# A two-block transformer on one core: the DeltaNet gate z projected in the first two head groups, half of the branch gates in the last two, expert places in another order

## Chip, cores and metric

The kernel runs on one core of one Trainium2 chip. The metric is the device time of one execution in microseconds (us). The engines are PE (TensorE, matrix products), DVE (VectorE), ACT (ScalarE), POOL (GpSimd) and SP (SyncE, which here issues the loads).

## What is computed

A sequence of 256 tokens of width 1024 goes through two blocks, then the experts. All in fp32. The first block (a short convolution, cross attention to a memory, SwiGLU, then block attention with the same) is not touched. The second block, in which the change lies, is:

```python
h = rms_norm_2(x, g_mix[l]) * (1.0 + sc1) + sh1
proj = h @ w_in[l]
dn_qkv, dn_z, dn_b, dn_a, c_q, c_kv, k_r, gates = jnp.split(proj, split_at, axis=-1)
y_dn = gated_deltanet_branch(dn_qkv, dn_z, dn_b, dn_a, ...) @ w_o_dn[l]
...
o = rms_norm_2(o, o_gain) * jax.nn.silu(zf)          # zf is dn_z, at the end of the DeltaNet branch
...
y_mla = mla_branch(c_q, c_kv, k_r, ...) @ w_o_mla[l]
g_dn, g_mla = jnp.split(jax.nn.sigmoid(gates), N_BRANCHES, axis=-1)
merged = g_dn * y_dn + g_mla * y_mla
x = x + gt1 * (merged @ w_out[l])
h = rms_norm_2(x, g_ffn[l]) * (1.0 + sc2) + sh2
x = x + gt2 * expert_choice_ffn(h, w_router[l], w_gate[l], w_up[l], w_down[l])
```

`dn_z` is 1024 wide, `gates` 2048. Both depend on `h` alone. `z` is needed when a DeltaNet head is finished; the gates are needed when the two branches are projected and merged. There are 16 experts with three matrices of 1024 x 1024 each.

## The kernel before

**Products.** Weights come in pieces of 128 x 1024 fp32 (0.5 MB). For every piece `stream` lets SP load it into `st` (line 140, three buffers), ACT casts it to the high part `wh` (line 144, four buffers), DVE subtracts to get the low part `wl` (line 146, three buffers), and PE makes three products for each pair of operands (`mm3`, lines 169 to 171): high by high, high by low, low by high. In `steps_as` a piece is 12 matmuls of 512 columns, in `steps_ws` 24 of 256. A tile scheduler orders the instructions of every engine before the run; each engine then works through its own list in order. Instructions issued under `b.first()` get a high priority.

**The second block's front** (`block2_front`) goes through six slots. Slots 0 to 3 project a group of DeltaNet heads each (`heads(slot)`, six pieces of `w_qkv` on the PSUM bank pair "M", transposes on the pair "A"; `head_in` convolves them on DVE, line 987). From slot 2 on the DeltaNet chains of earlier groups run beside them, `dn.group`, a row of short steps that inverts the 128 x 128 triangles, on the bank pairs "N0" and "N1". Slots 4 and 5 hold the queries of the second attention and, in the kernel before, `z`: `zsteps` is eight pieces of `w_z` on "M"; `put_z` (lines 1593 and 1594) takes a tanh on ACT and one DVE instruction for each of the four results of 128 x 512.

**The back** (`block2_back`) makes the keys and values of the second attention (`mla_keys`: `w_ukn` and `w_ukv`, two pieces each), then the attention over eight heads (`staged`: scores on "M", softmax, transposes, product with the values). All 16 pieces of `w_gt` are a filler here: `b.spare` holds their steps, on bank pair "A"; `b.fill(4)` takes four steps, `staged` two before the first head and two after each scores, and `b.fill(99)` the rest.

**Then** `block2_out` projects both branches (`w_odn`, `w_oml`), merges them with the gates, applies `w_out` and makes the router's logits `lg` (line 1712). `moe` picks the tokens and streams the experts' weights: 96 chunks of 2 MB (`Chunks`, `ex<-in_w_ex`), loaded by SP into 12 places of SBUF. Nine of the places (`FIRST`) are loaded early, during the back and the projections, as the memory they share with other tiles comes free; places 6 and 7 (pool `late`) and 8 later; from chunk 12 on a place is refilled in the order `TURN` when PE has used it (L1413).

Of the kernel before, what the change touches and what calls it, by code (L numbers as in the profile page):

```python
# [1261 lines left out]
def mla_keys(b, ckv, kr, c2):  # L1262
# [12 lines left out]
    nc.scalar.copy(krT, ps[:, :T])  # L1275
    b.fill(4)
    ck = [b.xp.tile([P, 2, T], F32R, tag=f"ck{i}", name=f"ck{i}") for i in range(2)]
# [253 lines left out]
def block2_front(b, x, mod, cos, sin):  # L1531
# [63 lines left out]

    zsteps = b.steps_as(h, b.stream("w_z"), 2, put_z, tag="M")
    chains = {}
    for slot in range(6):
        todo = []
        if slot >= 2:  # L1600
            todo.append(chains[slot - 2])
        if 1 <= slot <= 4:
            chains[slot - 1] = dn.group(2 * (slot - 1), grps[slot - 1], f"N{slot % 2}")
            todo.append(itertools.islice(chains[slot - 1], 6))
        if slot == 0:
            todo.append(dn.picks())
        if slot == 4:
            todo.append(mla_compressed(b, ckv, kr, cos, sin))
        if slot < 4:
            todo.append(heads(slot))  # L1610
        else:
            todo.append(queries if slot == 5 else itertools.islice(queries, 5))
            todo.append(zsteps if slot == 5 else itertools.islice(zsteps, 4))
        for _ in itertools.zip_longest(*todo):
            pass
    for n in range(4):
        dn.gate(2 * n, zs)
    for t in range(2):
        dn.o[t] = dn.o[t].rearrange("p h e -> p (h e)")
    return h, dn.o, ckv, kr, qnT, qrT  # L1620


def block2_back(b, mod, h, ckv, kr, qnT, qrT):

    nc = b.nc
    c2 = mod.c2
    sg = slot(b, 5, [2, 2 * D])
    sg = sg[:, 0], sg[:, 1]


    def put_g(t, nb, ps):
        nc.scalar.activation(sg[t][:, nb * 512:nb * 512 + 512], ps, AF.Tanh, scale=0.5)

    b.spare = b.steps_as(h, b.stream("w_gt"), 4, put_g)
    knT, krT, v = mla_keys(b, ckv, kr, c2)
    om = mla_attention(b, qnT, qrT, knT, krT, v, (2, 2))
    b.fill(99)
    y = b.kact()
    return y, om, sg
# [75 lines left out]
def block2(b, x, mod, out, wctx):  # L1715
    nc, I = b.nc, b.I
    pool = lambda ctx, name, bufs=1: ctx.enter_context(b.tc.tile_pool(name=name, bufs=bufs, reuse_waits="tile"))
    with ExitStack() as outer:
        b.kp = pool(outer, "kp")
        with ExitStack() as ctx:  # L1720
            b.phase(ctx, {"A": 2, "M": 2, "N0": 2, "N1": 2})
            cos, sin = b.trig2
            got = block2_front(b, x, mod, cos, sin)
# [11 lines left out]
        with ExitStack() as ctx:  # L1735
            for n in (6, 7):
                chunk.late[n] = ctx.enter_context(
                    b.tc.tile_pool(name=f"late{n}", bufs=1, side="right", reuse_waits="tile"))
            b.phase(ctx, {"E": 4, "Y": 2, "T": 2})
            b.ctx = ctx  # L1740
            moe(b, x, mod, out, chunk)
# [10 lines left out]

FIRST = (11, 0, 1, 10, 2, 3, 4, 9, 5)

TURN = (11, 0, 1, 2, 3, 4, 5, 6, 7, 8)

# [13 lines left out]
class Chunks:  # L1770
# [8 lines left out]
    def load(self, n):  # L1779
        b = self.b  # L1780
        src = b.I["w_ex"][self.n]
        i, self.n = self.n, self.n + 1
        if n == 11:
            return self.halves(i, src)
        pool = self.shot if n == 9 else self.late[n] if n in (6, 7) else b.kp if n in (3, 4) else b.slots
        st = pool.tile([P, 4, D], F32, tag=f"slot{n}", name=b.nm("ex"))
# [7 lines left out]
    def halves(self, i, src):  # L1794


        b = self.b
        pool, tags = (b.xp, b.slots), ("half", "slot11a")
        if i != 12:
            pool, tags = (b.slots, b.slots), ("slot11a", "slot11b")  # L1800
        res = []
# [10 lines left out]
    def __call__(self):  # L1812
        if self.got:
            return self.got.pop(0)
        if self.n < 12:
            return self.load(self.n - 3)
        return self.load(TURN[(self.n - 12) % 10])

# [45 lines left out]
```

## Time and profile before

| | |
|---|---|
| median of 3 runs | 1716.4 us (1715.72 to 1717.51) |
| the profiled execution | 1720.11 us |
| its span, first to last instruction | 1718.4 us |
| mean granted clock of PE, share of full speed | 0.95 |
| busy: PE, DVE, ACT | 1519.5 us, 888.0 us, 662.1 us |
| weight pieces through `stream` on DVE (L146) | 350, mean 1226 ns |

The profiled execution is 1.7 us longer than its span: what lies ahead of the first and behind the last instruction. A full clock of 1.00 is 2.4 GHz, and the lower level is 1.2 GHz, so a mean of 0.87 over a stretch says that the lower level was granted for a part of it.

### The profile page before, as it was taken

What the parts mean: (1) busy time and instruction counts of PE and PEld (TensorE: products, weight loads), DVE (VectorE), ACT (ScalarE), POOL (GpSimd) and SP (SyncE); (2) the same over time, 40 slices, a digit from 0 to 9 for tenths busy, and PEclk for the clock granted to TensorE, in tenths of its full rate; (3) what the DMA queues carried; (4) which work ended last, traced back from release to release, by engine and by line L of the source; (5) the groups of instructions that cost most, each with busy time, mean ns of one, the idle gap of its engine ahead of it and who ended that gap; (6) DMA issues with size and microseconds to landing.
All of it is one profiled execution on the core that took longest, in us unless ns stands there. A gap on an engine that the chain in (4) does not pass through costs nothing.

```text
span 1718.4 us, 25491 instructions
## 1 busy us (share of the span) xinstructions
PE 1519.5 (88%) x10150; PEld 1179.4 (69%) x10150; DVE 888.0 (52%) x1631; ACT 662.1 (39%) x1203; POOL 113.4 (7%) x146
## 2 busy tenths in 40 slices
PE   7999999999999999999879999999999866655654
PEld 7989899988888879999778888868764311212111
DVE  7665688787666555555778876555651200101001
ACT  6445554445455544444645544545321100000000
POOL 0000000000100000000261431100000000000000
PEclk9999999999999999999988999999999977878788
DMA  6565498886544535665422232467769999999997
GB/s 224 189 185 172 137 305 316 315 321 224 185 146 148 159 98 175 190 187 185 139 74 78 72 98 87 139 245 267 267 250 405 425 423 427 422 421 423 428 422 310
DMA packets 82790, 416.01 MB, mean 242 GB/s; under 512 B 9968, under 2 KB 11120, under 8 KB 70768
## 3 DMA queue, kind: packets, MB, share of 16 engines
q1 hardware_dynamic: 82672, 414.40, 66.0%
q8 instruction: 79, 1.29, 0.3%
q14 instruction: 39, 0.32, 0.1%
HBM read 413.32 MB, written 1.05 MB: 241 GB/s over the span
## 4 chain that ended last, share of the span: by engine, by line
PE 23%; DMA 21%; DVE 4%; POOL 2%; ACT 1%; issue 1%; SPq 0%; DVEq 0%; POOLq 0%; ACTq 0%
DMA ex<-in_w_ex 20%; PE ps L169 4%; PE ps L170 4%; PE ps L171 4%; PE ps L1413 3%; PE ps L1521 1%; PE ps L1095 1%; DVE wl L146 1%; PE ps L1335 1%; POOL dr L1040 1%; PE ps L1123 1%; PE ps L503 0%; PE ps L1334 0%; POOL YT L1107 0%; DMA st<-in_w_gt 0%
## 5 line engine op out<-in xcount | busy, mean ns | idle before, releaser
L146 DVE TENSOR_TENSOR wl<-st,wh 128x1024 fp32r<-128x1024 f32 x350 | 428.2, 1226 | 251.8 <-PE ps L171 99.5
L144 ACT CAST wh<-st 128x1024 fp32r<-128x1024 f32 x350 | 367.2, 1051 | 423.9 <-PE ps L170 134.6
L171 PE MATMUL ps<-ah,wl 128*128 128x256 f32 x1152 | 323.6, 281 | 3.4 <-DVE wl L146 3.4
L169 PE MATMUL ps<-ah,wh 128*128 128x256 f32 x1152 | 323.1, 281 | 0.1
L170 PE MATMUL ps<-al,wh 128*128 128x256 f32 x1152 | 322.6, 280 | 0.4 <-DVE al L190 0.4
L171 PEld LDWEIGHTS ps<-ah,wl 128*128 128x128 f32 x1152 | 216.6, 188 | 5.6 <-DVE wl L146 5.4
L169 PEld LDWEIGHTS ps<-ah,wh 128*128 128x128 f32 x1152 | 216.3, 188 | 2.7 <-ACT wh L144 0.5
L170 PEld LDWEIGHTS ps<-al,wh 128*128 128x128 f32 x1152 | 216.1, 188 | 2.6 <-DVE al L190 0.6
L1413 PE MATMUL ps<-ex,slot 128*32 128x512 f32 x768 | 130.1, 809 | 92.0 <-DMA ex<-in_w_ex 92.0
L1413 PEld LDWEIGHTS ps<-ex,slot 128*32 128x32 f32 x768 | 24.6, 130 | 191.8 <-DMA ex<-in_w_ex 147.2
L1370 DVE TENSOR_TENSOR room<-room,ps 128x512 f32<-128x512 f32 x8 | 5.5, 688 | 219.5 <-PE ps L1413 219.5
L1413 PE MATMUL ps<-ex,room 128*32 128x256 f32 (+1 forms) x768 | 71.5, 509 | 37.8 <-DMA ex<-in_w_ex 37.8
L1369 ACT ACTIVATE room<-ps 128x512 f32<-128x512 f32 x8 | 4.8, 597 | 258.7 <-PE ps L1413 258.7
L169 PE MATMUL ps<-wh,ah 128*128 128x512 f32 x256 | 102.3, 400 | 0.4 <-ACT sk L351 0.4
L171 PE MATMUL ps<-wh,al 128*128 128x512 f32 x256 | 101.5, 396 | 0.0
L170 PE MATMUL ps<-wl,ah 128*128 128x512 f32 x256 | 101.4, 396 | 0.0
L1413 PEld LDWEIGHTS ps<-ex,room 128*32 128x32 f32 x768 | 25.0, 117 | 83.1 <-DMA ex<-in_w_ex 39.6
L836 DVE SCALAR_TENSOR_TENSOR sm<-sm,csil 128x1024 f32<-128x1024 f32 x48 | 58.7, 1223 | 27.0 <-DMA sm<-in_w_mod 25.3
L169 PE MATMUL ps<-wh,yh 128*128 128x512 f32 x176 | 69.6, 395 | 0.1
L170 PE MATMUL ps<-wl,yh 128*128 128x512 f32 x176 | 69.4, 394 | 0.0
L171 PE MATMUL ps<-wh,yl 128*128 128x512 f32 x176 | 69.4, 394 | 0.0
L171 PE MATMUL ps<-wh,ak 128*128 128x512 f32 (+1 forms) x160 | 64.0, 401 | 1.4 <-DVE ak L1553 1.4
(533 smaller groups left out, 2561.1 us busy)
## 6 DMA issues: line engine op xcount, KB each, us to landing
ex<-in_w_ex SPq DMA_DIRECT2D x85, 2048.0 KB, 28.3
st<-in_w_ff SPq DMA_DIRECT2D x132, 512.0 KB, 3.6
sm<-in_w_mod SPq DMA_DIRECT2D x48, 512.0 KB, 5.2
ex<-in_w_ex SPq DMA_DIRECT2D x22, 1024.0 KB, 34.3
st<-in_w_ci SPq DMA_DIRECT2D x24, 512.0 KB, 3.6
st<-in_w_qkv SPq DMA_DIRECT2D x24, 512.0 KB, 3.4
st<-in_w_mk SPq DMA_DIRECT2D x16, 512.0 KB, 3.5
st<-in_w_mv SPq DMA_DIRECT2D x16, 512.0 KB, 3.5
```

Of the source, the lines that this page charges most:

```text
L144: nc.scalar.copy(hi[:, :w], st[:, q, :w])
L146: e.tensor_tensor(lo[:, :w], st[:, q, :w], hi[:, :w].bitcast(F32), ALU.subtract)
L169: mm(ps, lh[0], rh[0], start=start, stop=False)
L170: mm(ps, lh[0], rh[1], start=False, stop=False)
L171: mm(ps, lh[1], rh[0], start=False, stop=stop)
L836: nc.vector.scalar_tensor_tensor(st, st, 1.0, self.sc, ALU.mult, ALU.mult, accum_out=m[:, k:k + 1])
L1040: nc.gpsimd.tensor_tensor(r, ms, gs, ALU.mult)
L1095: nc.tensor.matmul(ps[:, s - s0], self.pick[:, s], xs, start=True, stop=True)
L1123: nc.tensor.matmul(p2[:, m], z[:, m], n1[:, m], start=True, stop=True)
L1335: nc.tensor.matmul(sc[:, t], qrT[r, hd // 2, s], krT[r], start=False, stop=True)
L1413: b.nc.tensor.matmul(ps[32 * j:32 * j + 32], lhs[:, 32 * j:32 * j + 32], w[:, j], start=k == 0, stop=k == KC - 1)
L1521: nc.tensor.matmul(ps, x[t][:, c * P:(c + 1) * P], pk[:, h, t, s], start=t == 0, stop=t == 1)
```

## The change

`z` is projected in slots 0 and 1, four steps (pieces) in each, on the bank pair "N0", which the DeltaNet chains do not use before slot 2. The first half of the gates takes the place of `z` in slots 4 and 5, on "M". The other half stays filler in the back, now also on "M", with `fill(2)` ahead of the keys, none before the first head and one after each scores. The gates' result `sg` gets a pool of its own (`sgp`, on the right side of SBUF) from the start of block two to the end of the projections, where it had been in place 5 of the experts. So the places are reordered: eight early ones, late ones 11, 6 and 7, then 8; the place loaded in halves is 0 where it was 11; `TURN` follows.

```diff
@@ -1273,7 +1273,7 @@
         nc.tensor.transpose(ps[:, t * P:(t + 1) * P], kr2[:, t].rearrange("p a d -> p (a d)"), b.eye)
     krT = b.xp.tile([P, T], F32, tag="krT", name="krT")
     nc.scalar.copy(krT, ps[:, :T])
-    b.fill(4)
+    b.fill(2)
     ck = [b.xp.tile([P, 2, T], F32R, tag=f"ck{i}", name=f"ck{i}") for i in range(2)]
     b.transpose_in(ckv, lambda c, ps: b.split(ck[0], ck[1], ps, c2[:, 76:78]), kc=2, tag="N")
     b.proj_ws(ck, b.stream("w_ukn"), 8,
@@ -1593,7 +1593,14 @@
         nc.scalar.activation(z, ps, AF.Tanh, scale=0.5)
         nc.vector.scalar_tensor_tensor(z, z, 1.0, ps, ALU.add, ALU.mult)
 
-    zsteps = b.steps_as(h, b.stream("w_z"), 2, put_z, tag="M")
+
+    sg = b.sgp.tile([P, 2, 2 * D], F32, tag="sg", name="sg")
+
+    def put_g(t, nb, ps):
+        nc.scalar.activation(sg[:, t, nb * 512:nb * 512 + 512], ps, AF.Tanh, scale=0.5)
+
+    zsteps = b.steps_as(h, b.stream("w_z"), 2, put_z, tag="N0")
+    gsteps = b.steps_as(h, b.stream("w_gt"), 4, put_g, tag="M")
     chains = {}
     for slot in range(6):
         todo = []
@@ -1606,34 +1613,28 @@
             todo.append(dn.picks())
         if slot == 4:
             todo.append(mla_compressed(b, ckv, kr, cos, sin))
+        if slot < 2:
+            todo.append(itertools.islice(zsteps, 4))
         if slot < 4:
             todo.append(heads(slot))
         else:
             todo.append(queries if slot == 5 else itertools.islice(queries, 5))
-            todo.append(zsteps if slot == 5 else itertools.islice(zsteps, 4))
+            todo.append(itertools.islice(gsteps, 4))
         for _ in itertools.zip_longest(*todo):
             pass
     for n in range(4):
         dn.gate(2 * n, zs)
     for t in range(2):
         dn.o[t] = dn.o[t].rearrange("p h e -> p (h e)")
-    return h, dn.o, ckv, kr, qnT, qrT
-
-
-def block2_back(b, mod, h, ckv, kr, qnT, qrT):
-
-    nc = b.nc
+    return h, dn.o, ckv, kr, qnT, qrT, gsteps, (sg[:, 0], sg[:, 1])
+
+
+def block2_back(b, mod, h, ckv, kr, qnT, qrT, gsteps, sg):
+
     c2 = mod.c2
-    sg = slot(b, 5, [2, 2 * D])
-    sg = sg[:, 0], sg[:, 1]
-
-
-    def put_g(t, nb, ps):
-        nc.scalar.activation(sg[t][:, nb * 512:nb * 512 + 512], ps, AF.Tanh, scale=0.5)
-
-    b.spare = b.steps_as(h, b.stream("w_gt"), 4, put_g)
+    b.spare = gsteps
     knT, krT, v = mla_keys(b, ckv, kr, c2)
-    om = mla_attention(b, qnT, qrT, knT, krT, v, (2, 2))
+    om = mla_attention(b, qnT, qrT, knT, krT, v, (0, 1))
     b.fill(99)
     y = b.kact()
     return y, om, sg
@@ -1717,6 +1718,7 @@
     pool = lambda ctx, name, bufs=1: ctx.enter_context(b.tc.tile_pool(name=name, bufs=bufs, reuse_waits="tile"))
     with ExitStack() as outer:
         b.kp = pool(outer, "kp")
+        b.sgp = wctx.enter_context(b.tc.tile_pool(name="sgp", bufs=1, side="right"))
         with ExitStack() as ctx:
             b.phase(ctx, {"A": 2, "M": 2, "N0": 2, "N1": 2})
             cos, sin = b.trig2
@@ -1733,7 +1735,7 @@
             chunk.early()
         wctx.close()
         with ExitStack() as ctx:
-            for n in (6, 7):
+            for n in LATE:
                 chunk.late[n] = ctx.enter_context(
                     b.tc.tile_pool(name=f"late{n}", bufs=1, side="right", reuse_waits="tile"))
             b.phase(ctx, {"E": 4, "Y": 2, "T": 2})
@@ -1750,9 +1752,11 @@
 WARM2 = (512, 512, 512)
 TAIL = {5: (512,)}
 
-FIRST = (11, 0, 1, 10, 2, 3, 4, 9, 5)
-
-TURN = (11, 0, 1, 2, 3, 4, 5, 6, 7, 8)
+FIRST = (0, 1, 10, 5, 9, 2, 3, 4)
+
+LATE = (11, 6, 7)
+
+TURN = (0, 1, 5, 2, 3, 4, 11, 6, 7, 8)
 
 
 def columns(w, f):
@@ -1780,9 +1784,9 @@
         b = self.b
         src = b.I["w_ex"][self.n]
         i, self.n = self.n, self.n + 1
-        if n == 11:
+        if n == 0:
             return self.halves(i, src)
-        pool = self.shot if n == 9 else self.late[n] if n in (6, 7) else b.kp if n in (3, 4) else b.slots
+        pool = self.shot if n in (5, 9) else self.late[n] if n in LATE else b.kp if n in (3, 4) else b.slots
         st = pool.tile([P, 4, D], F32, tag=f"slot{n}", name=b.nm("ex"))
         src = src.rearrange("p (e f) -> p e f", e=4)
 
@@ -1795,9 +1799,9 @@
 
 
         b = self.b
-        pool, tags = (b.xp, b.slots), ("half", "slot11a")
+        pool, tags = (b.xp, b.slots), ("half", "slot0a")
         if i != 12:
-            pool, tags = (b.slots, b.slots), ("slot11a", "slot11b")
+            pool, tags = (b.slots, b.slots), ("slot0a", "slot0b")
         res = []
         for f in range(2):
             st = pool[f].tile([P, 4, 512], F32, tag=tags[f], name=b.nm("ex"))
@@ -1813,7 +1817,7 @@
         if self.got:
             return self.got.pop(0)
         if self.n < 12:
-            return self.load(self.n - 3)
+            return self.load((LATE + (8,))[self.n - 8])
         return self.load(TURN[(self.n - 12) % 10])
```

(A last hunk halves a scratch area for DMA descriptors from 1024 to 512.)

Three places in the orders of the instructions. First DVE in slot 0, around the end of the DeltaNet gates (`dgt`, `g`, `gr`); `cv` is the convolution of a head group, `wl` the low part of a piece, `zs` is z. Before:

```order
L146 TENSOR_TENSOR wl_8955<-st_8953,wh_8956 128x1024
L916 TENSOR_TENSOR dgt<-dgt 128x32
L917 TENSOR_SCALAR dgt<-dgt 128x32
L987 SCALAR_TENSOR_TENSOR cv_8836<-ps_8811,cols_2232,cv_8836 128x254
L918 TENSOR_TENSOR dgt<-dgt 128x32
L1008 TENSOR_SCALAR k_1447_8700<-k_1447_8700 128x2
L987 SCALAR_TENSOR_TENSOR cv_8836<-ps_8811,cols_2232,cv_8836 128x255
L919 SCALAR_TENSOR_TENSOR dgt<-dgt 128x32
```

and with the change (of the four `wl`, 8867, 8938 and 8987 are pieces of `w_qkv`, 8916 one of `w_z`):

```order
L921 TENSOR_SCALAR g<-dgt 128x32
L184 TENSOR_TENSOR gr_8666<-g,gr_8665 128x32
L1181 TENSOR_SCALAR small_10029<-eg 128x4
L1181 TENSOR_SCALAR small_10632<-eg 128x4
L146 TENSOR_TENSOR wl_8867<-st_8865,wh_8868 128x1024
L146 TENSOR_TENSOR wl_8916<-st_8914,wh_8917 128x1024
L146 TENSOR_TENSOR wl_8938<-st_8936,wh_8939 128x1024
L146 TENSOR_TENSOR wl_8987<-st_8985,wh_8988 128x1024
L987 SCALAR_TENSOR_TENSOR cv_8896<-ps_8871,cols_2232,cv_8896 128x254
L987 SCALAR_TENSOR_TENSOR cv_8896<-ps_8871,cols_2232,cv_8896 128x255
L1594 SCALAR_TENSOR_TENSOR zs<-zs,ps_8701 128x512
```

Before, low parts, convolutions and gates alternate; now four low parts stand in a row behind the gates and ahead of the next convolution, and z's own DVE instruction stands among the convolutions.

Second, DVE in the back, where the low parts of `w_ukn`, `w_ukv` and `w_gt` are made (`ck` is the compressed key in two parts, `st<-ps` the first head's softmax). With the change 11909 is the second piece of `w_ukn`, 11945 and 11967 are `w_ukv`, and 12014 to 12194 are five pieces of the gates:

```order
L146 TENSOR_TENSOR wl_11909<-st_11907,wh_11910 128x1024
L146 TENSOR_TENSOR wl_11945<-st_11943,wh_11946 128x1024
L190 SCALAR_TENSOR_TENSOR ck_11863<-ps_11864,cols_2232,ck_11862 128x256 x2
L146 TENSOR_TENSOR wl_11967<-st_11965,wh_11968 128x1024
L146 TENSOR_TENSOR wl_12014<-st_12012,wh_12015 128x1024
L146 TENSOR_TENSOR wl_12058<-st_12056,wh_12059 128x1024
L146 TENSOR_TENSOR wl_12106<-st_12104,wh_12107 128x1024
L146 TENSOR_TENSOR wl_12150<-st_12148,wh_12151 128x1024
L146 TENSOR_TENSOR wl_12194<-st_12192,wh_12195 128x1024
L365 TENSOR_REDUCE st_11992<-ps_11986 128x2
```

Before, the same list has the two of `w_ukn`, two of `w_ukv` and three of the gates ahead of that row. On PE the change also reorders this place: the products with `w_ukv` and with the gates' pieces 12014 and 12058 come ahead of those with `w_ukn`, because the gates and `w_ukn` now share the pair "M".

Third, PE at the end of the attention (`p` and `pts` are a head's weights, L488 transposes them, L503 is the product with the values; 11882 and 11883 are banks of the gates). Before:

```order
L503 MATMUL ps_12287<-pts_12280,slot_11660 128x256
L488 MATMUL ps_12292<-c_eye,p_12271 128x128 x4
L503 MATMUL ps_12287<-pts_12280,slot_11660 128x256
L171 MATMUL ps_11883<-wh_11905,ak_8494 128x512
L169 MATMUL ps_11882<-wh_11936,ak_8494 128x512
L170 MATMUL ps_11882<-wl_11935,ak_8494 128x512
L503 MATMUL ps_12300<-pts_12293,slot_11660 128x256 x2
L171 MATMUL ps_11882<-wh_11936,ak_8494 128x512
```

and with the change (L1653 transposes the finished DeltaNet output, the last rows are the first of `w_odn`):

```order
L503 MATMUL ps_12290<-pts_12283,slot_11815 128x256 x2
L488 MATMUL ps_12295<-c_eye,p_12274 128x128 x4
L503 MATMUL ps_12303<-pts_12296,slot_11815 128x256 x2
L1653 MATMUL ps_12318<-c_eye,qo 128x128 x4
L1653 MATMUL ps_12327<-c_eye,qo 128x128 x4
L169 MATMUL ps_12354<-wh_12359,ak_12308 128x512
L170 MATMUL ps_12354<-wl_12358,ak_12308 128x512
```

Before, products of the gates stand between the last heads' steps and 118 more follow; now no product stands between the last three heads' steps, and the projection of the DeltaNet branch follows at once.

## Rows read from the trace of the kernel before

**Rows 1.** The page: busy time by engine, and shares of the last chain by engine.

```profile
PE 1519.5 (88%) x10150; PEld 1179.4 (69%) x10150; DVE 888.0 (52%) x1631; ACT 662.1 (39%) x1203; POOL 113.4 (7%) x146
...
PE 23%; DMA 21%; DVE 4%; POOL 2%; ACT 1%; issue 1%; SPq 0%; DVEq 0%; POOLq 0%; ACTq 0%
```

**Rows 2.** The chain that ended last: start us, us, what.

```profile
1351.86 28.19 DMA ex<-in_w_ex
...
1707.40 1.11 PE ps L1413 x16
```

**Rows 3.** Stretches: us, busy us (count) by engine, then clock, DMA share, GB/s.

```profile
848.00:876.00 28.00, 23.39 (x164) 22.42 (x162) 24.07 (x73) 15.94 (x46) 6.83 (x11) 0.88 0.41 131
876.00:914.00 38.00, 30.43 (x201) 29.20 (x202) 28.56 (x73) 17.23 (x48) 23.51 (x24) 0.87 0.22 71
914.00:999.00 85.00, 80.30 (x775) 74.74 (x775) 71.10 (x198) 44.83 (x122) 25.22 (x29) 0.96 0.24 75
999.00:1106.00 107.00, 100.21 (x817) 85.93 (x816) 69.84 (x150) 54.81 (x122) 29.06 (x31) 1.00 0.30 95
1106.00:1172.00 66.00, 65.19 (x305) 47.26 (x304) 33.82 (x67) 32.49 (x77) 1.23 (x2) 1.00 0.64 234
1172.00:1271.00 99.00, 97.02 (x444) 78.17 (x443) 55.69 (x64) 39.63 (x50) 0.00 (x0) 1.00 0.73 264
...
1351.00:1708.00 357.00, 220.98 (x1562) 62.09 (x1558) 25.81 (x52) 9.44 (x18) 2.21 (x3) 0.82 1.00 420
```

**Rows 4.** The same columns just ahead of the experts' steady stream.

```profile
1285.00:1290.00 5.00, 5.00 (x38) 2.03 (x40) 1.24 (x4) 0.46 (x1) 0.00 (x0) 0.50 0.04 14
```

**Rows 5.** PE in time, last w_out product and first expert product.

```profile
1270.19 0.40 PE L171 MATMUL ps<-wh,slot 128*128 128x512 f32 x1
...
1286.64 5.80 PE L1413 MATMUL ps<-ex,xe 128*32 128x512 f32 x36
```

**Rows 6.** SP queue in time: loads of the late places, then the halves.

```profile
1263.38 8.04 SPq L1791 DMA_DIRECT2D ex<-in_w_ex  x3
1275.64 13.54 SPq L1806 DMA_DIRECT2D ex<-in_w_ex  x2
```

**Rows 7.** PE in time, gates' products in the back.

```profile
1106.78 0.39 PE L171 MATMUL ps<-wh,ak 128*128 128x512 f32 x1
...
1117.24 0.39 PE L171 MATMUL ps<-wh,ak 128*128 128x512 f32 x1
```

**Rows 8.** DVE groups in slots 0 and 1: busy us, mean ns, then idle before.

```profile
L146 DVE TENSOR_TENSOR wl<-st,wh 128x1024 fp32r<-128x1024 f32 x12 | 14.7, 1228 | 1.8 <-PE ps L171 1.6
```

**Rows 9.** Tile zs: count, ns min/median/max, first and last start.

```profile
L1593 ACT ACTIVATE zs<-ps x4: 576/596/598, 1042.8 to 1085.1; 128x512 f32<-128x512 f32 x4
L1594 DVE SCALAR_TENSOR_TENSOR zs<-zs,ps x4: 680/682/687, 1043.9 to 1086.0; 128x512 f32<-128x512 f32 x4
```

**Rows 10.** PE in time, slot 0, behind a wait.

```profile
856.55 0.43 PE L169 MATMUL ps<-ak,wh 128*128 128x256 f32 x1 [2.85 <-DVE dgt L916]
...
858.06 0.41 PE L170 MATMUL ps<-ak,wh 128*128 128x256 f32 x1
...
860.28 0.28 PE L170 MATMUL ps<-ak,wh 128*128 128x256 f32 x1
...
860.99 0.28 PE L170 MATMUL ps<-ak,wh 128*128 128x256 f32 x1
```

**Rows 11.** DVE groups in the second attention.

```profile
L365 DVE TENSOR_REDUCE st<-ps 128x2 f32<-128x512 f32 x8 | 5.4, 691 | 6.0 <-PE ps L1335 6.0
L371 DVE TENSOR_SCALAR p<-p,st 128x256 f32<-128x256 f32 x16 | 4.9, 350 | 0.2
...
L494 DVE COPY pts<-ps 128x256 f32<-128x256 f32 x8 | 3.4, 424 | 1.1 <-ACT pts L493 1.0
```

**Rows 12.** ACT groups in the back.

```profile
L367 ACT ACTIVATE p<-ps,st 128x256 f32<-128x256 f32 x16 | 7.4, 472 | 1.7 <-DVE st L365 1.4
```

**Rows 13.** DVE in time, the logits.

```profile
1275.19 0.38 DVE L1712 SCALAR_TENSOR_TENSOR lg<-ps,ss,lc 128x16 f32<-128x16 f32 x2 [1.17 <-PE ps L1707]
```

More of the change, by code (lines that the diff above doesn't have):

```diff
@@ L1853 @@
     from concourse.bass_utils import run_bass_kernel_spmd as run
-    nc = bacc.Bacc("TRN2", target_bir_lowering=False, num_devices=1, dynamic_dma_scratch_size=1024)
+    nc = bacc.Bacc("TRN2", target_bir_lowering=False, num_devices=1, dynamic_dma_scratch_size=512)
     arrays = {f"in_{k}": v for k, v in pack(inputs).items()}
```

## The prediction

> **What bounds the kernel now.** I began with the page: PE is busy 88% of the span, and in the chain that ended last PE has 23% and DMA 21% [rows 1]. So one must ask where which of them holds. The end of the chain [rows 2] is read next: from the row at 1351.86, a load of an expert's chunk that PE waited 28.19 us for, to 1707.40 it consists almost wholly of such loads (11 of them), and PE only uses what lands. The stretches say the same [rows 3]: from 1351 to 1708 the DMA share is 1.00 at 420 GB/s. Ahead of it stands an order of bounds: in the back (1106:1172) PE is busy 65.19 of 66 us at clock 1.00, in the projections (1172:1271) 97.02 of 99; there PE is the bound, and DMA has room (0.64, 0.73). In slots 0 and 1 (848:876 and 876:914) neither is: PE is busy 23.39 + 30.43 = 53.8 of 66 us at a mean clock of 0.88 and 0.87, DVE 24.07 + 28.56 = 52.6.
>
> The two halves of the kernel meet between 1270 and 1290 [rows 4, 5]. The last w_out product ends at about 1270.6, the routing follows, the first expert product starts at 1286.64, and only then places come free. Between 1285 and 1290 DMA is nearly idle (0.04) since all twelve places are full. The next load, the second of the two halves in SP's queue, is out at 1275.64 + 13.54 = 1289.2 [rows 6], 18.6 us after the last w_out product. From there the end is a fixed time of loading away: (1707.4 − 1289.2) us at 420 GB/s is 176 MB, 84 chunks of 2.1 MB, which no early place holds before nor after the change. What PE saves ahead of 1270 shows at the end one for one, as long as the places are full by then; 4 us of DMA idleness is the slack [rows 4].
>
> **What the back loses.** Eight of its 16 gate pieces leave: 8 x 12 = 96 matmuls of 512 columns. In the back such matmuls follow each other at (1117.24 − 1106.78)/45 = 0.232 us [rows 7] at the full level of 2.4 GHz. 96 x 0.232 = **−22.3 us**, in a stretch that PE holds for 99%.
>
> **What the back gets in exchange.** Those products were cover. (a) The three low-part buffers: PE now uses w_ukv and two gate pieces ahead of w_ukn, whose two low parts wait in two of the three buffers; each of the next three pieces must go through the third. Its low part takes 1.23 us on DVE [rows 8], of which one high-by-high product (0.23) hides a part: about 1.0 x 3 = 3 us. (b) Gates, w_ukn and scores share the pair "M", so a bank changes hands after a tanh of 0.60 us (z's of the same shape [rows 9]) and a start of the next product: two blocks, some 0.75 each, 1.5 us. (c) The attention's end: no filler stands between the steps of the last heads. The softmax of a head is a row: 0.69 reduce, two exps of 0.47, two scalings of 0.35, a copy of 0.42 [rows 11, 12], 2.8 us, with reciprocal and transposes over 3. Before, gate products covered it; now that of the last head is covered only by the product of the head ahead. Then 8 transposes of the DeltaNet output and their split wait for nothing but PE. I take 4.5 us. (d) Loads: the back's missing 22 us were also time for early chunks. Two chunks now stand back to back in the w_odn pieces and three in w_oml. A piece takes PE 12 x 0.232 = 2.8 us; at 420 GB/s its 0.5 MB takes 1.25 us. In the about 45 us of both projections, 16 pieces and five chunks ask 16 x 1.25 + 5 x 5 = 45 us of DMA: just enough, 0 to 4 us lost, 1 taken. Sum of (a) to (d): **+10 us**; between 5 (if (a) and half of (c) are hidden) and 14 (all of (c) and (d) at their worst).
>
> **What slots 0 and 1 get.** z's 96 matmuls (22.3 us at the full level), 8 casts on ACT, 8 low parts on DVE (8 x 1.23 = 9.8) and four of put_z (4 x 0.68 = 2.7 [rows 9]): DVE +12.5 us. Here the cost cannot be read off, only bounded. DVE: 52.6 + 12.5 = 65.1 of 66, so with perfect packing nothing is added, and if every instruction is simply appended, 12.5. PE: 53.8 + 22.3 = 76.1, 10 over the 66; but the 53.8 contain stretches at the lower level. Behind a wait of 2.85 us for DVE a matmul of 256 columns takes (858.06 − 856.55)/7 = 0.216 us, and (860.99 − 860.28)/6 = 0.118 later, with PE dense in between [rows 10]: the two levels, 1.2 and 2.4 GHz. If z fills such waits the clock stays up and 53.8 shrinks to 53.8 x 0.875 = 47, with z 69.4: 3.4 over. And slot 2 onward has 4.7 us of PE idle (914:999 [rows 3]) for the chains, which may take up some of a delay. So 0 to 12.5; I take **+6**, in the middle, nearest to PE dense at a clock between.
>
> The Trainium skill, "TensorE: Matmul & The Clock Gate", section "HAM oscillation — how this bites in real kernels", says that idle gaps of PE bring the clock down, and that work after each gap starts cold. The slowed rows behind the 2.85 us wait agree [rows 10]; by it z's products would be the cheaper the better they fill, and x would be nearer to 3.4.
>
> **What I cost at nothing.** Slots 4 and 5 exchange eight pieces for eight of the same form on the same banks; put_z's 2.7 us leave DVE, which is busy 69.84 of 107 there and not the bound (PE 100.21 [rows 3]). The memory of the gates: from slot 4 to the end of w_out, a pool of its own. The places: late ones 11, 6, 7 instead of 6, 7. Before, they were issued at 1263.38 [rows 6], 7 us ahead of the end of w_out. Place 7 now overlaps tiles that the logits still read (L1712, done at 1275.19 + 0.38, 5 us after the last w_out product [rows 13]), and 8 is queued behind it in SP; 2 chunks of 5 us each, then, done about 16 us after w_out, when the first free place comes at 18.6. Cover: 2 us; if it is gone, up to 4 us of loading are late at the end.
>
> **The sum.** −22.3 + 10 + 6 = −6.3, taken as −6.4. Profiled: 1720.1 − 6.4 = 1713.7. The median of before stands 3.7 below its profiled execution, so 1716.4 − 6.4 = **1710.0 us**. With the ends: −22.3 + 5 + 0 = −17 and −22.3 + 14 + 12.5 = +4, so 1699 to 1720.5. A change of less than 0.2% (3.4 us) cannot be told from none.
>
> **Rivals.**
> 1. *The back's whole gain comes through* (y = 5, x near 0): some 1700 us. For it: PE is dense in the back, and DVE's total fits in slots 0 and 1. Against: in-order queues never pack perfectly; in slot 0 four low parts stand in a row ahead of a convolution, 4.9 us in which heads' results wait.
> 2. *DVE takes the place of PE as bound in slots 0 and 1*: 12.5 us appended, −22.3 + 10 + 12.5 = +0.2, so 1716.6, no change. For it: 52.6 of 66 busy already, and the waits of PE there are for DVE [rows 10].
> 3. *Sharing "M" makes PE stop and start in the back*, so that the clock falls there as it has in slots 0 and 1. About 54 us of back would remain (66 − 22 + 10), at a mean of 0.87 instead of 1.00: + 8, so −6.4 + 8 = +1.6, 1718. In the back before, the gates already cycled through the two banks of "A" and the clock stayed at 1.00 [rows 3]; that speaks against it.
> 4. *Slower: z runs at the lower level.* Slots 0 and 1 are where PE is granted 1.2 GHz for long stretches. If z's products come in the pauses and don't raise the clock, each costs 2 x 0.216 = 0.43, 96 of them 41.4 us against 12.2 us of PE idleness: x = 29 and −22.3 + 10 + 29 = +17, 1733 at the utmost; at half of that excess 1724. It decides from x above 12.3. Against it: behind the wait the low level lasted from 856.55 to before 860.28 only, while PE stayed dense [rows 10].
>
> The Trainium skill has rival 3 as a rule: same page, "A second HAM failure mode: psum-queue depth-cycling", by which cycling through PSUM banks let PE idle briefly between groups and the clock oscillate. The trace does not show it in this kernel's back.
>
> **How the numbers follow.** The sum above 0.50; rival 1 0.10; rival 2 0.17; rival 3 0.08, of which 0.03 is slower by over 3.4 us; rival 4 0.15. So faster 0.60, same 0.17 + 0.05 = 0.22, slower 0.15 + 0.03 = 0.18. The range leaves out the best part of rival 1 and the upper half of rival 4: 1701 to 1721; the likeliest case's own is 1704 to 1714.
>
> **What would show it.** In the stretches of the changed kernel the back, from the end of slot 5 to the first w_odn product, should be 12 us shorter; PE's waits there should name DVE wl (a) and the softmax (c). Slots 0 and 1 should last about 72 us in place of 66, with DVE above 90% and a clock above 0.88. The last w_out product should end 6 us earlier, and DMA idle 4 us or less ahead of the first free place. The prediction is wrong if the delay of slots 0 and 1 is given back in slots 2 and 3 (then faster), if their clock is at or under 0.87 (rival 4), or if DMA is still loading the late places when the first place comes free.

## The result, and the profile after the change

The changed kernel takes 1732.63 us, median of three executions (1729.97 to 1735.41), beside 1716.4 before: ratio 1.0093, 95% interval 1.0075 to 1.0111. It is slower by 16 us where 6 less were forecast, and lies above the range. Run again beside the later experiments it took 1730.52 us, 1.0072 (1.0049 to 1.0095) of the kernel before on the same chip.

The page of the changed kernel, the same row as the first of [rows 1]:

```profile
PE 1527.2 (88%) x10150; PEld 1175.8 (68%) x10150; DVE 893.6 (52%) x1631; ACT 663.3 (38%) x1203; POOL 113.4 (7%) x146
```

Matmuls and weights are the same in number; PE is busy 8 us longer and the span is 15.3 us longer (1733.7). To see where, the second block is cut at the same six points of the program in both traces: the end of the last product with w_b0 (the start of slot 0), of the 12th and of the 24th piece of w_qkv (slots 0 and 1, slots 2 and 3), of the last w_uqn (slots 4 and 5), the start of the first w_odn product (the back), the end of the last w_out product (the projections) and the end of the span (the tail). The ends come from the trace's rows, counted off against the order of the program. Lengths in us, with the experiments that are told below:

| | start of slot 0 | slots 0, 1 | slots 2, 3 | slots 4, 5 | back | projections | tail |
|---|---|---|---|---|---|---|---|
| before | 847.9 | 65.8 | 85.4 | 104.1 | 92.5 | 74.9 | 447.8 |
| after | 848.8 | 80.1 | 94.6 | 103.5 | 78.1 | 79.7 | 448.9 |
| after, again (e5) | 846.3 | 80.0 | 95.6 | 102.0 | 78.1 | 78.0 | 448.5 |
| e1, no z | 849.0 | 66.0 | 92.0 | 103.5 | 78.1 | 79.8 | 450.0 |
| e2, init on N1 | 851.9 | 70.4 | 97.0 | 101.9 | 78.1 | 82.8 | 446.8 |
| e3, z without DVE | 848.5 | 69.9 | 92.6 | 102.6 | 78.1 | 78.2 | 449.6 |
| e4, z alone | 844.9 | 79.3 | 99.1 | 84.7 | 92.2 | 75.4 | 445.5 |
| e6, last step late | 846.8 | 79.2 | 87.5 | 100.1 | 87.9 | 78.2 | 446.7 |
| e7, e2 and e6 | 847.6 | 69.2 | 86.7 | 100.1 | 92.1 | 78.2 | 448.2 |
| e8, gates on A | 845.3 | 78.5 | 99.1 | 101.9 | 73.6 | 77.9 | 449.9 |
| e9, e2, last step split | 848.2 | 69.1 | 86.7 | 101.5 | 78.1 | 78.6 | 449.0 |
| e10, e9 and e8 | 847.0 | 70.8 | 86.7 | 102.0 | 73.5 | 78.1 | 446.1 |
| e11, e2 and e8 | 845.3 | 69.2 | 96.9 | 101.9 | 73.6 | 78.0 | 449.1 |
| e12, places alone | 847.0 | 65.6 | 84.0 | 104.1 | 92.8 | 76.9 | 447.5 |

So the back did get shorter, by 14.4 us, and slots 4 and 5 cost nothing, as forecast. But slots 0 and 1 are 14.3 us longer, slots 2 and 3 9.2, the projections 4.8, and the tail and the start of slot 0 about 1 each. The stages of the changed kernel, and four short windows within them (columns as in [rows 3]; the first row begins 0.9 us ahead of slot 0):

```profile
847.94:928.88 80.94, 72.00 (x455) 64.10 (x455) 64.78 (x162) 42.65 (x102) 22.50 (x25) 0.94 0.42 136
928.88:1023.53 94.65, 84.20 (x796) 78.21 (x795) 79.72 (x199) 47.98 (x132) 34.46 (x38) 0.96 0.19 63
1023.53:1127.06 103.53, 98.54 (x790) 84.24 (x789) 64.58 (x140) 51.36 (x111) 27.85 (x31) 0.98 0.32 99
1127.06:1205.12 78.06, 70.76 (x327) 49.31 (x326) 36.89 (x71) 37.90 (x89) 1.22 (x2) 1.00 0.49 175
1205.12:1284.80 79.68, 75.53 (x340) 60.07 (x340) 43.66 (x54) 27.17 (x34) 0.00 (x0) 0.98 0.74 282
...
855.00:865.00 10.00, 4.63 (x26) 3.65 (x24) 7.64 (x33) 4.09 (x14) 2.04 (x3) 0.77 0.26 92
865.00:870.00 5.00, 5.00 (x13) 3.94 (x13) 0.48 (x3) 0.54 (x4) 2.69 (x3) 0.50 0.00 0
...
990.00:1000.00 10.00, 6.13 (x42) 5.93 (x40) 7.45 (x18) 1.38 (x2) 5.72 (x6) 0.85 0.01 2
1000.00:1010.00 10.00, 9.58 (x132) 9.00 (x132) 7.28 (x15) 4.42 (x12) 0.42 (x1) 0.81 0.17 52
```

Before the change PE was idle for 12 of 66 us in slots 0 and 1, most of it in four waits (us in total, times, longest):

```profile
PE ps L1041 <- POOL dr L1040: 3.5, 1, 3.5
PE ps L1095 <- DVE x L1089: 3.4, 1, 3.4
PE ps L169 <- DVE dgt L916: 2.9, 1, 2.9
PE ps L960 <- DVE g L921: 1.5, 1, 1.5
```

z has filled the first two of them, not those that name `dgt` and `g`. With the change PE is idle for 8.9 of 80.9 us there, and more than half of that lies in one place: 5.4 us of 855 to 865. Behind it the granted clock is 0.50, all at the lower level. That place on PE, then the one in slots 2 and 3 (start us, us, what; in brackets the idle time ahead and what ended it):

```profile
861.09 0.66 PE L996 MATMUL ps<-c_eye,qkT 128*128 128x128 f32 x2 [2.55 <-DVE dgt L917]
863.18 0.60 PE L960 MATMUL ps<-g,m_le 128*128 128x8 f32 x2 [1.43 <-DVE g L921]
...
864.91 0.77 PE L169 MATMUL ps<-wh,ak 128*128 128x512 f32 x1
865.48 0.63 PE L170 MATMUL ps<-wl,ak 128*128 128x512 f32 x1
...
869.75 0.63 PE L171 MATMUL ps<-wh,ak 128*128 128x512 f32 x1
...
996.88 3.67 PE L1123 MATMUL ps<-n,YT 128*128 128x64 f32 x16 [3.87 <-DVE n L1120]
```

and the same two places on DVE:

```profile
869.99 1.23 DVE L146 TENSOR_TENSOR wl<-st,wh 128x1024 fp32r<-128x1024 f32 x1 [4.20 <-PE ps L170]
...
990.94 3.08 DVE L1250 SCALAR_TENSOR_TENSOR qo<-qo,f,zs 128x128 f32<-128x128 f32 x4 [0.99 <-POOL f L1242]
993.94 0.85 DVE L1074 SCALAR_TENSOR_TENSOR AT<-ps,br,IN 128x128 f32<-128x128 f32 x3
...
996.16 0.67 DVE L1120 TENSOR_TENSOR n<-ps,m_lev 128x512 f32<-128x512 f32 x1
```

*First place.* The products that start at 864.91 are z's first. Ahead of them PE has L960 to L963, the four small products of the DeltaNet's start, which wait for `g`, the end of a row of small DVE instructions (`dgt`), and the transposes of a head (L996). The small products stand ahead because they use a bank of N0, and a block of z needs both. Three pieces of z had been loaded, cast and split by 857; their low parts fill the three buffers. So the third piece of w_qkv, cast at 856.9, gets no low part, and DVE, which is not busy, waits until PE has used a piece of z (4.20 us, "<-PE ps L170"). PE, which takes its list in order, waits as well, and starts z at the lower level: (869.75 − 865.48)/10 = 0.427 us for a matmul, against 0.232 in [rows 7].

*Second place.* L1250 is the last step of the DeltaNet heads, which multiplies by f and z. As z is now finished by slot 1, the scheduler has put the first four of them into DVE's list as soon as the first chain ends, in the middle of the next chains. They wait for POOL (f, the head's scale), run for 3.08 us, and behind them stand L1074 and L1120 of the chains, for which PE waits 3.87 us; the clock is then 0.85 and 0.81 of full. Before the change the wait for the same instruction (L1123) is short, and L1250 starts only at 1047.5:

```profile
978.77 1.44 PE L1123 MATMUL ps<-n,YT 128*128 128x64 f32 x11 [0.24 <-DVE n L1120]
```

```profile
L1250 DVE SCALAR_TENSOR_TENSOR qo<-qo,f,zs x16: 332/345/720, 1047.5 to 1110.0; 128x128 f32<-128x128 f32 x16
```

and after it, in the same view (count, ns min/median/max, first and last start):

```profile
L1250 DVE SCALAR_TENSOR_TENSOR qo<-qo,f,zs x16: 335/347/1127, 990.9 to 1134.0; 128x128 f32<-128x128 f32 x16
```

*The projections.* ACT waits longer for loads there (us in total, times, longest), before and after:

```profile
ACT wh L144 <- DMA st<-in_w_oml: 7.1, 5, 5.3
```

```profile
ACT wh L144 <- DMA st<-in_w_oml: 16.3, 7, 5.2
```

For w_odn they were 5.8 us and are 7.1. DMA moves 282 GB/s there, 249 before. But PE waits for none of these casts. It is idle for 4.1 of 79.7 us, where it had been idle for 1.6 of 74.9, and its longest waits are for DVE to finish with results of PE's own products:

```profile
PE ps L1696 <- DVE x L1677: 1.8, 1, 1.8
PE ps L254 <- DVE sg L1666: 0.9, 1, 0.9
```

The rest is PE busy for 2.2 us more, at a clock of 0.98 in place of 1.00. So the loads are heavier, but it is not shown that PE loses its time to them.

*The tail* is 1.1 us longer, within the 445.5 to 450.0 of the other runs. The slack of [rows 4] is used up: as far behind the last w_out product, DMA has a share of 0.84 where it had 0.04.

```profile
1300.00:1305.00 5.00, 5.00 (x50) 1.47 (x49) 0.75 (x3) 0.00 (x0) 0.00 (x0) 1.00 0.84 306
```

*The back* is shorter by less than the 22.3 us of its products, and PE, at clock 1.00, now waits where it had cover:

```profile
PE ps L170 <- DVE wl L146: 1.3, 2, 0.7
...
PE ps L1334 <- ACT sg L1600: 0.7, 1, 0.7
PE ps L503 <- DVE slot L184: 0.6, 1, 0.6
PE ps L503 <- DVE pts L494: 0.5, 1, 0.5
...
PE ps L503 <- DVE st L365: 0.5, 1, 0.5
```

### The profile page after: what moved, and what is told of

Read it like the earlier page. It is cut to its first block, busy times and chain, and to the rows that moved or that the text cites. A ratio compares the mean times of both kernels' runs of the same rounds, so it can differ in the third digit from the quotient of the medians.

```text
span 1733.7 us, 25471 instructions
## 1 busy us (share of the span) xinstructions
PE 1527.2 (88%) x10150; PEld 1175.8 (68%) x10150; DVE 893.6 (52%) x1631; ACT 663.3 (38%) x1203; POOL 113.4 (7%) x146
## 5 line engine op out<-in xcount | busy, mean ns | idle before, releaser
L170 PE MATMUL ps<-al,wh 128*128 128x256 f32 x1152 | 323.1, 281 | 0.4 <-DVE al L190 0.4
L170 PEld LDWEIGHTS ps<-al,wh 128*128 128x128 f32 x1152 | 216.3, 188 | 2.6 <-DVE al L190 0.6
L1413 PE MATMUL ps<-ex,room 128*32 128x256 f32 (+1 forms) x768 | 78.1, 553 | 37.0 <-DMA ex<-in_w_ex 37.0
L171 PE MATMUL ps<-wh,al 128*128 128x512 f32 x256 | 101.5, 396 | 0.0
L170 PE MATMUL ps<-wl,ah 128*128 128x512 f32 x256 | 101.3, 396 | 0.0
L170 PE MATMUL ps<-wl,yh 128*128 128x512 f32 x176 | 69.5, 395 | 0.0
L171 PE MATMUL ps<-wh,yl 128*128 128x512 f32 x176 | 69.4, 394 | 0.0
L170 PE MATMUL ps<-wl,ak 128*128 128x512 f32 (+1 forms) x160 | 64.4, 403 | 1.3 <-DVE wl L146 1.3
```

Source lines behind the costliest of these rows:

```text
L170: mm(ps, lh[0], rh[1], start=False, stop=False)
L171: mm(ps, lh[1], rh[0], start=False, stop=stop)
L1413: b.nc.tensor.matmul(ps[32 * j:32 * j + 32], lhs[:, 32 * j:32 * j + 32], w[:, j], start=k == 0, stop=k == KC - 1)
```

## The experiments

Single executions of one kernel spread over up to 14 us here (e2), and the start of slot 0, ahead of which nothing is changed, lies between 844.9 and 851.9. So medians are given with the kernel before on the same chip, and causes are read from the stages, which repeat better: two profiles of the changed kernel differ by at most 1.7 us in a stage. Each stage comes from one profile, though, and its clock differs from run to run. A first theory was that the shared bank of N0 holds up z and with it the head projections (A), with two others against it: DVE is the bound there (B, rival 2), or PE is simply full (C).

**e1, z left out.**

```diff
-    zsteps = b.steps_as(h, b.stream("w_z"), 2, put_z, tag="N0")
+    nc.gpsimd.memset(zs, 1.0)
...
-        if slot < 2:
-            todo.append(itertools.islice(zsteps, 4))
```

> The changed kernel without the projection of z (zs is set to a constant, w_z is not loaded), so its output lacks z. Every theory that puts the loss on z in slots 0 and 1 expects the last head convolution (L987) back near 1001 us, where it is 1026.8 with the change, and 22 to 26 us off the time: 1707 to 1711 us. If some 10 of the 25 us of delay come from elsewhere (the new pool for the gates, the gates in slots 4 and 5), only 12 to 16 us: 1717 to 1721.

1715.78 us, 0.9982 (0.9970 to 0.9995) of before. Slots 0 and 1 are back at 66.0, so all of their loss is z's. But slots 2 and 3 stay at 92.0, 6.6 more than before, without a product of z, and the time is 5 us above the 1707 to 1711 that z in slots 0 and 1 alone would give. What is left of z in this kernel is that it is ready early. PE's longest wait there is 4.1 us for the same instruction of DVE (n, L1120). From this came theory D, the second place above.

**e2, the DeltaNet's first products on N1.**

```diff
         self.eg, self.es = sm("eg"), sm("es")
-        ps = b.psum("N0")
+        ps = b.psum("N1")
```

> The changed kernel with the DeltaNet's first four small products (L960 to L963) on bank pair N1 in place of N0. Theory A (a shared bank): z's first products can't start before those, which wait for g; until then z's three loaded pieces hold the three low-part buffers and the head projections stand still. Then this edit gives back the stall of PE at 857 to 863 (5.5 us) and the low clock behind it (about 2.6 us), and what the chains lose by it later: 1722 to 1726 us, with PE granted 1.00 at 860 to 870. Theory B (DVE is the bound of slots 0 to 3, rival 2 of the prediction): the order of banks changes nothing, 1730 to 1734. Theory C (PE is simply full there, z costs what its products cost): 1730 to 1734 too, with PE over 95% busy in both.

1720.1 us, 1.0013 (0.9997 to 1.0029); 2 us faster than the expected 1722 to 1726. Slots 0 and 1 take 70.4 us in place of 80. z's first product now runs at the start of slot 0, ahead of `g`; two rows of PE, then the stage:

```profile
852.00 0.39 PE L169 MATMUL ps<-wh,ak 128*128 128x512 f32 x1
...
867.10 0.29 PE L960 MATMUL ps<-g,m_le 128*128 128x8 f32 x2
```

```profile
851.90:922.30 70.40, 67.07 (x450) 60.42 (x449) 64.34 (x160) 41.48 (x100) 23.63 (x25) 1.00 0.45 153
```

The clock is 1.00 and PE is busy for 95%. The name of one pair of banks is worth 9.6 us there. Theory C, which expected no gain, falls with it. (The 82.8 us of the projections in e2's profile, its slowest execution, have a clock of 0.94.)

**e3, z without DVE.**

```diff
-                lo = self.wp.tile([P, PIECE], F32R, tag="wl", name=self.nm("wl"), bufs=3)
+                if name != "w_z":
+                    lo = self.wp.tile([P, PIECE], F32R, tag="wl", name=self.nm("wl"), bufs=3)
...
+                if name == "w_z":
+                    yield hi[:, :w], hi[:, :w]
+                    continue
                 e.tensor_tensor(lo[:, :w], st[:, q, :w], hi[:, :w].bitcast(F32), ALU.subtract)
...
-        nc.vector.scalar_tensor_tensor(z, z, 1.0, ps, ALU.add, ALU.mult)
```

> The changed kernel in which z needs no DVE: the low part of w_z is left out (its product uses the high part again, so PE has the same work) and so is the second step of z's activation. 12.5 us of DVE work go from slots 0 and 1, and z takes no low-part buffer. Theory B (DVE bound): 12 us and more come back, 1717 to 1721. Theory A: the head projections get their buffers back, so the stall of 5.5 us goes in part, but z still waits for g: 1725 to 1729. Theory C: no change, 1730 to 1734.

1719.56 us, 1.0011 (0.9998 to 1.0024). Its time is the one that B expected, but e2, which keeps all of DVE's work, is as fast, and that B had excluded. So the stage decides:

```profile
848.50:918.40 69.90, 67.24 (x451) 60.66 (x451) 55.23 (x151) 41.16 (x101) 20.67 (x25) 1.00 0.45 159
```

DVE is busy for 9.1 us less than in e2, and the stage is no more than 0.5 us shorter: DVE is not what bounds it (against B). z's first product stands behind `g` here too (861.92 us, L960 at 861.00), so a late z alone costs next to nothing. What e3 and e2 have in common is that the head projections get their low parts in time. Low-part buffers for z alone, with its DVE work kept, were not tried.

**e4, z alone.** The kernel before with z on N0 in slots 0 and 1 and nothing in its place in slots 4 and 5.

```diff
-    zsteps = b.steps_as(h, b.stream("w_z"), 2, put_z, tag="M")
+    zsteps = b.steps_as(h, b.stream("w_z"), 2, put_z, tag="N0")
...
+        if slot < 2:
+            todo.append(itertools.islice(zsteps, 4))
...
-            todo.append(zsteps if slot == 5 else itertools.islice(zsteps, 4))
```

> The kernel before with one part of the change: z on N0 in slots 0 and 1, nothing in its place in slots 4 and 5, all gates in the back as before, places as before. If z in slots 0 and 1 causes the loss alone: L987 ends near 1026 as with the change, slots 4 and 5 get shorter by z's 22 us less what their own chains and queries need, some 15 us, the back is that of before: 1716 + 25 - 15 = 1726, between 1719 and 1730. If the loss needs the other parts (the gates in slots 4 and 5, the pool): 1712 to 1717.

1724.82 us, 1.0044 (1.0031 to 1.0057), near the 1726 that z alone would give. The loss in slots 0 to 3 needs z alone (79.3 and 99.1). Slots 4 and 5 get 19.4 us shorter, so z's 22.3 us of products were nearly all on the path there too. Of the 99.1 us a part is the clock, 0.91 there where the changed kernel has 0.96.

**e5, the changed kernel again.** No edit.

> The changed kernel itself, run again beside the other variants, since single executions here spread over some 10 us. 1728 to 1735 us; if the median is under 1726 the first three executions were high ones and all differences to it shrink by as much.

1730.52 us, 1.0072 (1.0049 to 1.0095): as expected, the loss is there again, and its stages are within 1.7 us of the first profile's.

**e6, the heads' last step behind the last chain.**

```diff
-        nc.gpsimd.tensor_tensor(ss, ss, self.qs[:, :, hs], ALU.add)
-        nc.gpsimd.tensor_tensor(ss, ss, b.mhalf.to_broadcast([P, 2, 2]), ALU.pow)
+        if h0 == 6: nc.gpsimd.tensor_tensor(self.f, self.f, self.qs, ALU.add)
+        if h0 == 6: nc.gpsimd.tensor_tensor(self.f, self.f, b.mhalf.to_broadcast([P, 2, 8]), ALU.pow)
```

> The changed kernel with the factor f of all head groups made once, behind the last chain, so that the last step of the heads (L1250, 16 DVE instructions that need f and z) can only run there; with z ready early it had come at 991 us, four DVE instructions that wait for POOL (f L1242) in front of the next chain's. Theory D (z ready early lets the heads' last step into DVE's queue, where it holds up the chains): PE's wait for n (L1120) of 3.9 us and the low clock behind it go, slots 2 and 3 get 5 to 8 us shorter, in all 5 to 9 us less than the changed kernel. Rival (slots 2 and 3 are longer because their chains start later against the heads): no difference over 2 us.

1727.1 us, 1.0049 (1.0034 to 1.0064), 3.4 less than e5: less than expected. Slots 2 and 3 do as theory D said, 87.5 in place of 95.6, and PE has no wait for n of over 0.4 us left. But the back is 9.8 us longer. The view of L1250 shows all sixteen in one place, at the back's beginning:

```profile
L1250 DVE SCALAR_TENSOR_TENSOR qo<-qo,f,zs x16: 342/342/352, 1121.7 to 1125.6; 128x128 f32<-128x128 f32 x16
```

**e7, the edits of e2 and e6 together.**

> Both: the DeltaNet's first products on N1 and the heads' last step behind the last chain. If theories A and D are two separate costs, their gains add up: 15 to 20 us less than the changed kernel, 1712 to 1718 us, slots 0 to 3 at 160 to 165 us in all where they take 151 before and 175 with the change. If they are the same delay seen twice, no more than 12 us less: 1719 to 1723.

1721.36 us, 1.0017 (1.0001 to 1.0033): short of the expected gain. By the time alone A and D would be one delay, for which 1719 to 1723 was expected. The stages say otherwise: slots 0 to 3 take 155.9 us, less than the 160 to 165 expected of two costs; the back takes 92.1 and eats the rest. DVE there, then PE's clock further on in the back:

```profile
1111.73 4.29 DVE L1250 SCALAR_TENSOR_TENSOR qo<-qo,f,zs 128x128 f32<-128x128 f32 x16 [2.88 <-POOL f L1242]
```

```profile
1145.00:1155.00 10.00, 8.16 (x18) 4.15 (x18) 4.75 (x13) 3.72 (x14) 0.00 (x0) 0.56 0.47 190
1155.00:1165.00 10.00, 10.00 (x31) 6.96 (x30) 3.17 (x8) 2.51 (x8) 0.00 (x0) 0.59 0.00 0
```

The sixteen and their wait for POOL, 7.2 us, stand in front of the low parts of w_ukn and w_ukv. In these 20 us of the attention the clock is near the lower level; in e6 the back has 0.94 in place of e7's 0.89, and is 4.2 us shorter. So a fix of the second place can itself cost as much as the place had.

**e8, the back's gates on A.**

```diff
-    gsteps = b.steps_as(h, b.stream("w_gt"), 4, put_g, tag="M")
+    wgt = b.stream("w_gt"); gsteps = b.steps_as(h, wgt, 2, put_g, tag="M")
+    gback = b.steps_as(h, wgt, 2, lambda t, nb, ps: put_g(t, nb + 2, ps))
...
-    return h, dn.o, ckv, kr, qnT, qrT, gsteps, (sg[:, 0], sg[:, 1])
+    return h, dn.o, ckv, kr, qnT, qrT, gback, (sg[:, 0], sg[:, 1])
```

> The changed kernel with the back's gate pieces on bank pair A, as before the change, and no longer on M beside w_ukn and the scores. Terms (a) and (b) of the prediction (order of low parts 3 us, banks that change hands 1.5 us) say that the back gets 3 to 5 us shorter and the time 3 to 5 us less than the changed kernel's. If these terms are not what the back loses, it stays at 78 us and the time within 2 us.

1727.36 us, 1.0047 (1.0028 to 1.0066), 3.2 less than e5, as expected. The back takes 73.6 us, 4.5 less. Slots 2 and 3, which the edit does not touch, take 3.5 us more, at a clock of 0.91 where e5 has 0.95; on N1 the same edit gains 4.5 (e2 to e11) and 4.6 us (e9 to e10) in the back.

**e9, the last step in two portions**, with e2's edit. These lines stand in place of the two of POOL that e6 changed:

```diff
+        fs = {4: slice(0, 6), 6: slice(6, 8)}.get(h0)
+        if fs: ...
```

> As the run before with both edits, but f is made in two portions, for the first three head groups behind the third chain and for the last behind the fourth, so that twelve of the sixteen L1250 run in slot 5, where DVE has room, and only four in the back. If the 14 us that the back lost there came from all sixteen standing in front of the low parts of w_ukn and w_ukv, the back is at 78 to 80 us again, slots 0 to 3 stay at 156 us, and the time is 1711 to 1716 us. If slots 4 and 5 lose what the back gains: 1720 to 1724.

1713.26 us, 0.9973 (0.9961 to 0.9986), as expected: faster than the kernel before. Back and slots 2 and 3 are both short at once (78.1 and 86.7), and slots 4 and 5 pay 1.4 us against e7.

**e10, e9 with the gates on A.**

> The same with the back's gates on bank pair A. All costs found so far taken away but those of loading: slots 0 and 1 at 69, 2 and 3 at 87, 4 and 5 at 101, back 74, projections 78, and the last 448: 1707 to 1712 us, faster than both kernels. If the gains don't add up: 1715 to 1719.

1708.09 us, 0.9944 (0.9930 to 0.9958): as expected, faster than both kernels. Its stages up to the end of the back:

```profile
847.00:917.80 70.80, 67.08 (x450) 60.44 (x450) 64.39 (x160) 41.54 (x100) 23.66 (x25) 1.00 0.45 153
917.80:1004.50 86.70, 79.72 (x786) 73.70 (x785) 76.50 (x195) 46.73 (x126) 34.12 (x36) 1.00 0.22 74
1004.50:1106.50 102.00, 99.42 (x801) 85.12 (x800) 65.14 (x145) 52.86 (x116) 27.85 (x29) 0.98 0.29 97
1106.50:1180.00 73.50, 69.67 (x330) 49.67 (x328) 36.10 (x71) 35.97 (x87) 1.23 (x2) 1.00 0.52 196
```

Slots 0 and 1, at 0.87 and 0.88 in [rows 3], run at 1.00 here: z fills the pauses. By its page PE is busy for 1512.2 us, 15 less than in the changed kernel, for the same 10150 matmuls.

**e11, e10 without the late last step.**

> DeltaNet's first products on N1 and the back's gates on A, the heads' last step left where the changed kernel has it. If that step (theory D) costs 8 us in slots 2 and 3 by itself, this is 5 to 8 us slower than the run with all three edits: 1714 to 1718. If it is nothing by itself: within 2 us of it.

1716.1 us, 0.9993 (0.9981 to 1.0006), 8.0 slower than e10, at the upper end of the expected 5 to 8: the step costs this by itself, and the stage has it, 96.9 against 86.7.

**e12, the places alone.** The order of places and the gates' pool as in the change; z in slots 4 and 5, all gates in the back.

> The change of the experts' places and of the gates' pool alone; z in slots 4 and 5 and all gates in the back as before. The prediction costs this at nothing, up to 4 us if the late places are late: 1716 to 1720 beside 1717 to 1719 for the kernel before, projections at 75 us. If the projections take 78 to 80 here too, the 4 us lost there belong to the order of places and not to the shorter back.

1721.38 us, 1.0021 (1.0004 to 1.0038), somewhat over the expected 1716 to 1720. The projections take 76.9, 2.0 more than before and 1 to 3 less than with the whole change. That points to the places for a part of their loss, but two profiles of the changed kernel differ by 1.7 us there, so it is barely shown. The span of its profiled execution, 1717.9, is 0.5 us under that of before; where the other 2 of the 4 us of its median go stays open.

## Why the prediction was wrong

**The step that failed** is "What slots 0 and 1 get": "So 0 to 12.5; I take +6". Measured in slots 0 to 3: +14.3 and +9.2, 23.5 us. Of the signs that it named, slots 0 and 1 were to last about 72 us with DVE busy above 90%; they lasted 80.1 with DVE at 80%. The bounds were made of sums of work, PE's and DVE's, against the length of the stage. Both terms that were missed are places in the queues, and neither shows in a sum:

- z's first block shared N0 with the DeltaNet's start, which waits for g, and its low parts took all buffers meanwhile: 9.6 us (e5 to e2; 10.0 from e6 to e7, 9.3 from e8 to e11). The order printed ahead of the prediction had it, four low parts in a row behind g; the text priced them as 4.9 us of DVE and did not ask what the row waits for.
- The consumer of z came early: 8.1 us (e5 to e6), 10.3 (e2 to e7), 10.2 (e11 to e10) in slots 2 and 3, of which PE's wait for n is 3.9 and a part the clock (0.95 in e11, 1.00 in e10). The prediction followed what z's products displace, and nowhere what a finished z releases. Slots 2 and 3 were even given as a place that "may take up some of a delay".

Without these two, slots 0 and 1 take 70.4 (e2) and slots 2 and 3 86.7 (e9): +4.6 and +1.3, together 5.9, where +6 was taken. That it meets so closely is partly luck: +6 was the middle of a range and meant slots 0 and 1 alone. These took 3.3 to 5.0 more in e2, e9, e10 and e11, with PE busy for 67 us at clock 1.00. That is the prediction's own bound for a clock that stays up, 69.4 us and "3.4 over", rather than the middle.

**What the back loses and gets.** (a), (b) and (c) were taken at 3, 1.5 and 4.5 us, 9 in all; the back lost 22.3 − 14.4 = 7.9. The sum was about right, the parts were not: PE waits for low parts (a) for 1.3 us, for a bank that the gates hold (b) for 0.7, at the attention's end (c) for 2.1 (1.6 ahead of L503, 0.5 ahead of L1653). With the gates on A (e8) the back loses 3.4; PE's waits in it are 3.8 us in all (1.8 before), none of them at the attention's end, the longest 1.07 for ck at the keys. So (c) too hung on the pair M, which costs 4.5 in all. That this equals (a) and (b) as forecast is luck. Loads (d) were taken at 1 us. The projections cost 3.1 (e5) to 4.8 more, but PE waits there for DVE and not for casts, so this is no term of the prediction, and why the waits arose stays open.

**What was costed at nothing.** Slots 4 and 5: right (−0.6 to −2.1). The places: at most 2.0 us in the projections (e12), where none was taken; the slack at the tail was used up, at no cost that the tail's spread would let one see.

**The sum with the measured terms**: −22.3 + 3.4 + 4.5 + 4.8 (projections) + 14.3 + 9.2 − 0.6 + 1.1 + 0.8 (start of slot 0) = +15.2; the spans differ by 15.3. It closes because the stages fill the span; it does not test the causes. With the two missed terms taken out, e9 is the change as it was reasoned about, and it is 3.9 us faster than before at the median where 6.4 were forecast.

**Readings of the prediction that were off.** The 28.19 us in the chain [rows 2] are the time of one load, not a wait of PE, whose longest for a chunk was 4.3 us; nothing is worked out from it. And 1106 to 1172 is not the whole back: up to the first w_odn product it lasted 92.5 us, with most of the 118 gate products behind 1172. So rival 3 had about 80 us to price at a clock of 0.87, not 54, which by its own working is 12 us, not 8.

**The rivals.** Rival 1's 1700 us was not reached by any run (1708.09 in e10): z's own cost remains. Rival 2 (DVE) is refuted by e2 and e3. Rival 3 is not seen: the back kept 1.00, though sharing the pair cost 4.5 us. The oscillation of the clock that the Trainium skill describes under "A second HAM failure mode: psum-queue depth-cycling" ("TensorE: Matmul & The Clock Gate") is not in this trace either: 1.00 over the 78.06 us of the back. Rival 4 gave a time that fits, 1724 to 1733, by a mechanism that does not: z ran at the lower level only from 864.9 to about 870, some 13 matmuls of 96 at 0.20 us too much, 2.6 us; the mean clock of the stage rose from 0.87 to 0.94. The Trainium skill's section "HAM oscillation — how this bites in real kernels" of the same page, by which idle gaps of PE bring the clock down, agrees with e2 and e10: where z fills the gaps, the stage is granted 1.00.

## What to carry to other kernels

Work moved into idle time is not paid by the idle time of its engine alone: ask what its first instruction waits for, which shared buffers and banks it holds during that wait, and who needs them. Then ask who is released earlier by its result; here the scheduler put that work into the next free place of an in-order queue, in front of what was critical there. Where executions spread more than the effect, cut the traces at the same points of the program and compare stages; here the stages of the variants added up, and three small edits turned a loss of 0.7 to 0.9% into a gain of 0.6%.

## What the runs showed of the hardware

The clock of PE can stay near its lower level while PE is busy: in e7 the two stretches of 10 us shown above were granted 0.56 and 0.59 with PE busy for 8.16 and 10.00 us, behind a wait of 1.84 us that ended at 1146.93. The first four L1250 of the changed kernel took 711, 1127, 1125 and 340 ns, where the median of all sixteen is 347; POOL worked on IN and dr (L1044, L1040) beside the first three, and was idle beside the fourth. The cause was not tested. POOL's power for f took 2.9 us for 128x16 elements and 1.0 for 128x4.
